# Sparse attention: probabilities times values as plain float32 products of 64 columns, in place of pairs of split fp32r products

## The chip, the cores and the metric

The kernel runs on one core of one Trainium2 chip. The metric is the device time of one execution in microseconds (us); three runs of the kernel before gave 2080.49, 2083.45 and 2084.88 us, so its median is 2083.45 us.

## The reference

Two blocks of a transformer are computed one after the other on 512 tokens of width 1024, in float32. The change lies in the second block, in one of its two mixers, the sparse attention (`nsa_mixer`). It has 16 query heads of 64 columns in 4 groups of 4; the heads of a group share keys and values. Each head's output is the gated sum of three attentions:

- over 31 compressed blocks of keys and values (padded to 32),
- over the selected blocks,
- over a window of 512 positions.

With 512 tokens the second and third both reach all earlier positions, so the kernel computes both as full causal attentions of 512 by 512 with the same bias, each with its own keys and values:

```
p   = softmax(q @ k.T / 8 + bias, over the keys s <= t)
out = gate_cmp * p_cmp @ v_cmp + gate_sel * p_sel @ v_sel + gate_win * p_win @ v_win
```

The other mixer (RWKV), the merge gates, the first block, the cross attention and the feed-forward networks are not touched.

## The kernel before, in words

Everything is held transposed: 128 channels on the partitions, 512 tokens along the free axis. Nearly every product that needs float32 accuracy is made on TensorE with the type fp32r, from operands that are split into a high part, rounded to fp32r by a ScalarE copy, and a low part, the rest, made by a VectorE subtraction. A weight product is then three fp32r matmuls: high by high, high by low, low by high (`gemm_g`, L243 to L245). Some small products are plain float32 matmuls instead: the bias tables (L973), the compression (L1013, L1097), the RWKV products (L744, L757, L874 to L891). Each of these shows as two matmul instructions in the trace; a transpose (L328) or an fp32r product shows as one.

The program is a number of phases. The one that matters here is called `pa2`; in the trace it runs from about 1050 to about 1500 us. Three generators are woven into one program order by `weave` (L57): each yields an estimate of its work, and the stream that is least far along goes next. The streams of `pa2` are the sparse attention (`nsa`), the RWKV chain with the merge behind it (`right`), and the last ten tiles of the merge gates (`merge_gates`, matmuls into `psg_m`). The yields, and so the weave, stand outside the edited lines. After that the build's scheduler moves instructions past each other on each engine; the order in the trace is therefore not that of the text (transposes of tile j+1 stand ahead of products of tile j, for instance). Each engine and each DMA queue then works strictly in the order that was built. When the attention stream has ended, the product of its output with a weight (`branch`, `psg_b`) follows, then the rest of the network.

The parts that the change touches:

- `nsa_compressed` (L1058, in the phase before) makes the compressed keys and values. The values stand in `vc`, for each of 4 groups 64 columns high part and 64 columns low part (L1098 on ScalarE, L1099 on VectorE).
- `nsa_pre` (L1112) makes, one group ahead, the queries, the keys of the selected branch, and the probabilities of the compressed branch. These are transposed on TensorE (L1150) and split into `pc`, high and low (L1151, by `split`, L162 and L163).
- `nsa_values` (L1155) loads, once for every two groups, the values of both branches: four transfers from `vd` into `ld` buffers, of which there are three, shared with the loads of queries and keys. ScalarE and VectorE then write the high and low parts side by side into `VT` (L1163, L1164), of which there is one buffer. The transfers are issued from GpSimd's queue (POOL), as are those of the bias (L1183), the queries and keys (L1052, L292) and the gates' weights (L209).
- `nsa_group` (L1166) runs 4 heads. A head starts its PSUM accumulator `o` (one bank) with two fp32r products of the compressed branch, 32 rows by 128 columns, 512 moving columns (L1188), and runs `attend` twice.
- `attend` (L299) is called by the sparse attention with a `gate` (32 times) and by the first block's attention without one (8 times). It makes the scores of four row blocks (L311, L312), adds the bias and takes the minimum on VectorE (L313), the exponential on ScalarE (L315), and scales the rows (L321, L323). Then, for each key tile j of 0 to 3, it transposes the probabilities (L328), copies them out of PSUM as fp32r (L330, ScalarE), subtracts for the low part (L331, VectorE) and multiplies both with `V(j)`, 128 stationary columns of which 64 are the value's high part and 64 its low part (L332, L333). The moving operand has 512, 384, 256 and 128 columns for the four j.
- `o_evac` (L335) adds the lower half of the accumulator to the upper: a ScalarE copy (L340) and a VectorE add (L341).

Of the kernel before, what the change touches and what calls it, by code (L numbers as in the profile page):

```python
# [8 lines left out]
F32 = mybir.dt.float32  # L9
# [29 lines left out]
class Gen:  # L39
# [259 lines left out]
    def attend(self, qst, kst, bias, V, o, first, last, gate=None):  # L299

        nc = self.nc
        kh, kl = kst
        st = self.f("sm", shape=(128, 32))
        m, s, r = st[:, 0:4], st[:, 4:8], st[:, 8:12]
        Pt = self.f("p", shape=(128, 1280))
        P = [Pt[:, 64 * i * (i + 1):64 * (i + 1) * (i + 2)] for i in range(4)]
        for i, pt in enumerate(P):
            w = 128 * (i + 1)
            ps = self.ps("a")
            qt = qst[:, i * 128:i * 128 + 128]  # L310
            nc.tensor.matmul(ps[:, :w], qt, kh[:, :w], start=True, stop=False)  # L311
            nc.tensor.matmul(ps[:, :w], qt, kl[:, :w], start=False, stop=True)  # L312
            nc.vector.tensor_tensor_reduce(pt, ps[:, :w], bias[:, 512 - w:], 1.0, 3e38, OP.add, OP.min,  # L313
                                           m[:, i:i + 1])
            nc.scalar.activation(pt, pt, AF.Exp, bias=m[:, i:i + 1], scale=-1.0, accum_out=s[:, i:i + 1])  # L315
        nc.vector.reciprocal(r, s)
        if gate is not None:
            nc.vector.tensor_tensor(r, r, gate, OP.mult)
        for i, pt in enumerate(P):
            if i >= 2:  # L320
                nc.scalar.activation(pt, pt, AF.Copy, scale=r[:, i:i + 1])  # L321
            else:
                nc.vector.tensor_scalar(pt, pt, r[:, i:i + 1], None, op0=OP.mult)  # L323
        for j in range(4):
            w = 512 - 128 * j
            ps = self.ps("b")
            for i in range(j, 4):
                nc.tensor.transpose(ps[:, (i - j) * 128:(i - j + 1) * 128], P[i][:, j * 128:j * 128 + 128], self.ident)  # L328
            ph, pl = self.f("pt", F32R), self.f("pt", F32R)
            nc.scalar.copy(ph[:, :w], ps[:, :w])  # L330
            nc.vector.tensor_tensor(pl[:, :w], ps[:, :w], ph[:, :w].bitcast(F32), OP.subtract)  # L331
            nc.tensor.matmul(o[:, j * 128:], V(j), ph[:, :w], start=first and j == 0, stop=False)  # L332
            nc.tensor.matmul(o[:, j * 128:], V(j), pl[:, :w], start=False, stop=last and j == 3)  # L333
# [724 lines left out]
    def nsa_compressed(self):  # L1058
        nc, A, V, S = self.nc, self.A, self.nc.vector, self.nc.scalar
        k = lambda n, w: self.rp.tile([128, w], F32R, name=n, tag=n, bufs=1)  # L1060
        self.cmp = kc2, vc = (k("kch", 128), k("kcl", 128)), k("vc", 512).rearrange("p (g s d) -> p g s d", g=4, s=2)
        self.gt = self.rp.tile([128, 4, 48], F32, name="gt", tag="gt", bufs=1)
        self.nsa_consts()
        yield 3.0
# [30 lines left out]
        for g in range(4):  # L1095
            for ct in range(2):
                nc.tensor.matmul(p[:, g], hx[ct][:, 128 * g:128 * g + 128], w2[:, ct, 128:192], start=ct == 0, stop=ct == 1)  # L1097
        S.copy(vc[:, :, 0], p)  # L1098
        V.tensor_tensor(vc[:, :, 1], p, vc[:, :, 0].bitcast(F32), OP.subtract)  # L1099
        yield 1.0  # L1100

    def norm_col(self, sq):
# [9 lines left out]
    def nsa_pre(self, g):  # L1112
# [35 lines left out]
        ps = self.ps("b")  # L1148
        for i in range(4):
            nc.tensor.transpose(ps[:, i * 128:i * 128 + 128], e[:, i * 128:i * 128 + 128], self.ident)  # L1150
        pc = self.split(ps, tag="pc")  # L1151
        yield 2.0
        return qst, kst, pc

    def nsa_values(self, gp):  # L1155
        nc, V, S = self.nc, self.nc.vector, self.nc.scalar
        VT = self.VT = self.f("vt", F32R, (128, 4 * 4 * 128)).rearrange("p (t k n) -> p t k n", t=4, k=4)
        for t2 in range(2):
            z = self.f("ld").rearrange("p (t k d) -> p t k d", t=2, d=64)
            for t in range(2):  # L1160
                self.side.dma_start(z[:, t].rearrange("p k d -> p (k d)"), self.vd[gp, 2 * t2 + t])
            v = VT[:, 2 * t2:2 * t2 + 2]
            S.copy(v[:, :, :, 0:64], z)  # L1163
            V.tensor_tensor(v[:, :, :, 64:128], z, v[:, :, :, 0:64].bitcast(F32), OP.subtract)  # L1164

    def nsa_group(self, g, qst, kst, pc):  # L1166

# [7 lines left out]
        for h in range(4):  # L1175
# [8 lines left out]
                                              ap=[[576, 2], [-1, 64], [1, 512]]))  # L1184
            o = self.ps("o")
            hs = slice(32 * h, 32 * h + 32)
            for i in range(2):
                nc.tensor.matmul(o, vc[hs, g].rearrange("p s d -> p (s d)"), pc[i][hs], start=i == 0, stop=False)  # L1188
            ready = self.nsa_pre(g + 1) if h == 3 and g < 3 else iter(())
            for br in (1, 2):  # L1190
                kv = 2 * (br - 1) + gl
# [3 lines left out]
                if br == 1:  # L1195
                    try:
# [1 line left out]
                            yield next(ready)  # L1198
                    except StopIteration as done:
                        pre = done.value  # L1200
            self.o_evac(O, o, par)
            if par == 1:
                pr = hd // 2
                nc.sync.dma_start(self.ynd[pr], O)
# [238 lines left out]
def emit(tc, A, out, dbg={}):  # L1443
    nc = tc.nc
    with ExitStack() as ctx:
# [14 lines left out]
        with g.phase("rec"):  # L1460
# [11 lines left out]
                g.weave(("", g.rwkv_fronts(xs), 245), ("_p", others(), 170))  # L1472
            g.banks = {"a": "01", "b": "23", "n": "2", "o": "4", "a_b": "5", "b_b": "6", "g_m": "7", "g_b": "56"}
            g.side = nc.gpsimd
            with g.phase("pa2", f=3, ld=3, qst=5, kst=6, p=2, pt=4, bias=2, pc=2, kz=1, o=1, ot=1, vt=1,
                         kb=1, v=1, bk=1, ys=1, vs=2, vu=2, yc=6, vgb=2, y=2, f_m=1, **{"as": 1}):
                g.reserve(kb=1024, v=512, vs=1024, vu=1024, yc=128, bk=1024, y=1024, ys=1024,
                          vgb=512, ld=512, kst=512, vt=2048, qst=512, f=512, pc=512, bias=512)

                live = {"", "_m"}  # L1480

# [146 lines left out]
```

## Time and profile before

| what | value |
|---|---|
| runs (us) | 2080.49, 2083.45, 2084.88; median 2083.45 |
| profiled execution | 2082.19 us, span of its instructions 2080.4 us |
| mean granted TensorE clock | 0.981 of full speed |
| TensorE matmul, busy | 2004.5 us (96%) |
| VectorE, busy | 1308.6 us (63%) |
| ScalarE, busy | 925.3 us (44%) |

The profile names the engines PE (TensorE matmul), PEld (its weight loads), DVE (VectorE), ACT (ScalarE), POOL (GpSimd) and SP (the queue that issues most transfers). Times are in us, means of single instructions in ns. Matmuls are pipelined: one may start while the one before still counts as busy, so the distance between two starts tells more of TensorE's load than the busy time. `128*128 128x512 f32` is a matmul with 128 rows and 128 columns of stationary operand and 512 moving columns; the trace writes f32 for fp32r operands of matmuls as well.

### The profile page before, as it was taken

The page shows a single profiled execution, that of the slowest core. Times are in us where ns is not written, and L with a number is a line of the kernel's source. Part 1 is how long each engine was busy: PE and PEld are TensorE (multiplying, and loading weights), DVE is VectorE, ACT ScalarE, POOL GpSimd, SP SyncE. Part 2 cuts the span into 40 slices and gives each one's busy share as a digit, 9 for nine tenths or more (in the row PEclk, how much of TensorE's full clock was granted, in tenths as well). Part 3 has the DMA queues.
Part 4 walks back from the last instruction along what each step waited for, and adds up shares of the span by engine and source line. Part 5 has one row for each costly group of instructions (what it writes and reads, how often), then busy time and mean ns, then how long its engine had stood idle before and what let it go on. Part 6 is the DMA issues. An engine that isn't in the chain of part 4 may idle for free.

```text
span 2080.4 us, 27852 instructions
## 1 busy us (share of the span) xinstructions
PE 2004.5 (96%) x9927; PEld 1627.0 (78%) x9927; DVE 1308.6 (63%) x3007; ACT 925.3 (44%) x1778; POOL 95.5 (5%) x167
## 2 busy tenths in 40 slices
PE   8999999999999899899988899999999999999999
PEld 7778888888888677777767687887878778888887
DVE  5785432554463568687848988888466756666522
ACT  4874531442254233333346577777243443333311
POOL 0000000000003200000120111000000000000000
PEclk9999999999999999999989899999999999999999
DMA  5222332333355754755673445446442123333332
GB/s 161 82 85 93 99 93 92 117 108 120 117 185 158 171 147 141 183 147 168 191 168 105 129 122 145 126 123 190 154 140 84 41 81 92 101 92 98 95 109 84
DMA packets 178267, 256.75 MB, mean 123 GB/s; under 512 B 95409, under 2 KB 109953, under 8 KB 178129
## 3 DMA queue, kind: packets, MB, share of 16 engines
q1 hardware_dynamic: 162832, 231.31, 38.2%
q0 software_dynamic: 15296, 23.66, 3.9%
q8 instruction: 79, 1.29, 0.3%
q14 instruction: 60, 0.48, 0.1%
HBM read 205.12 MB, written 45.53 MB: 120 GB/s over the span
## 4 chain that ended last, share of the span: by engine, by line
PE 46%; DVE 6%; ACT 3%; issue 2%; DMA 2%; SPq 0%; POOL 0%; DVEq 0%; ACTq 0%; POOLq 0%
PE psg L243 8%; PE psg L245 8%; PE psg L244 8%; PE psg_b L243 1%; PE psg_b L244 1%; PE psg_b L245 1%; PE psb L328 1%; DVE ys L777 1%; PE psg_p L243 1%; PE psg_p L244 1%; PE psg_p L245 1%; PE pso L332 1%; PE psa L744 1%; DVE ys L778 1%; PE pso L333 1%
## 5 line engine op out<-in xcount | busy, mean ns | idle before, releaser
L222 ACT CAST wh<-ws 128x1024 fp32r<-128x1024 f32 (+2 forms) x283 | 291.6, 1031 | 697.9 <-PE psg L244 457.1
L223 DVE TENSOR_TENSOR wl<-ws,wh 128x1024 fp32r<-128x1024 f32 (+2 forms) x283 | 339.4, 1201 | 266.3 <-ACT wh L222 265.7
L243 PE MATMUL psg<-xh,wh 128*128 128x512 f32 x984 | 392.2, 399 | 4.7 <-ACT wh L222 4.7
L245 PE MATMUL psg<-xh,wl 128*128 128x512 f32 x984 | 393.1, 399 | 0.0
L244 PE MATMUL psg<-act,wh 128*128 128x512 f32 x912 | 359.7, 395 | 1.1 <-DVE act L166 1.1
L243 PEld LDWEIGHTS psg<-xh,wh 128*128 128x128 f32 x984 | 186.0, 189 | 46.8 <-ACT wh L222 5.5
L245 PEld LDWEIGHTS psg<-xh,wl 128*128 128x128 f32 x984 | 186.0, 189 | 41.5 <-issue 1.2
L244 PEld LDWEIGHTS psg<-act,wh 128*128 128x128 f32 x912 | 171.1, 188 | 42.8 <-DVE act L166 1.5
L243 PE MATMUL psg<-act,wh 128*128 128x512 f32 x496 | 196.1, 397 | 2.8 <-ACT act L165 1.4
L245 PE MATMUL psg<-act,wl 128*128 128x512 f32 x496 | 196.1, 396 | 0.5 <-DVE wl L223 0.5
L244 PE MATMUL psg<-xl,wh 128*128 128x512 f32 x352 | 139.7, 397 | 0.0
L243 PEld LDWEIGHTS psg<-act,wh 128*128 128x128 f32 x496 | 92.8, 188 | 27.2 <-ACT act L165 2.2
L245 PEld LDWEIGHTS psg<-act,wl 128*128 128x128 f32 x496 | 93.0, 187 | 23.7 <-DVE wl L223 1.3
L315 ACT ACTIVATE p<-p,sm 128x128 f32<-128x128 f32 (+3 forms) x160 | 89.6, 561 | 15.0 <-DVE sm L313 13.6
L331 DVE TENSOR_TENSOR pt<-psb,pt 128x512 fp32r<-128x512 f32 (+3 forms) x160 | 75.8, 487 | 20.0 <-ACT pt L330 17.7
L244 PE MATMUL psg<-x,wh 128*128 128x512 f32 x216 | 88.2, 409 | 0.0
L313 DVE CUSTOM_DVE_ANT_0 p<-psa,bias 128x128 f32<-128x128 f32 (+3 forms) x160 | 75.9, 485 | 8.2 <-PE psa L312 6.1
L328 PE MATMUL psb<-ident,p 128*128 128x128 f32 x400 | 75.3, 285 | 2.5 <-DVE y L921 0.9
L244 PEld LDWEIGHTS psg<-xl,wh 128*128 128x128 f32 x352 | 66.3, 188 | 14.0
L330 ACT CAST pt<-psb 128x512 fp32r<-128x512 f32 (+3 forms) x160 | 65.8, 424 | 25.7 <-PE psb L328 20.8
L243 PE MATMUL psg_p<-xh,wh 128*128 128x512 f32 x176 | 73.3, 416 | 1.1 <-ACT f L957 0.6
L244 PE MATMUL psg_p<-x,wh 128*128 128x512 f32 x176 | 72.2, 410 | 0.0
(491 smaller groups left out, 3899.1 us busy)
## 6 DMA issues: line engine op xcount, KB each, us to landing
ws<-in_w_in SPq DMA_DIRECT2D x49, 512.0 KB, 4.0
ws<-in_w_fup SPq DMA_DIRECT2D x44, 512.0 KB, 3.5
ws<-in_w_up SPq DMA_DIRECT2D x32, 512.0 KB, 3.5
ws<-in_w_down SPq DMA_DIRECT2D x32, 512.0 KB, 3.6
ws<-in_w_fdn SPq DMA_DIRECT2D x16, 512.0 KB, 3.6
ws<-in_w_qku SPq DMA_DIRECT2D x12, 512.0 KB, 3.6
ws<-in_w_in POOLq DMA_DIRECT2D x10, 512.0 KB, 4.6
ws<-in_w_out SPq DMA_DIRECT2D x8, 512.0 KB, 3.5
```

What stands on the lines that cost most here:

```text
L222: nc.scalar.copy(wh[:, :n], ws[:, :n])
L223: nc.vector.tensor_tensor(wl[:, :n], ws[:, :n], wh[:, :n].bitcast(F32), OP.subtract)
L243: nc.tensor.matmul(p[:, :n], wh[:, s], h[:, :n], start=c + k == 0, stop=False)
L244: nc.tensor.matmul(p[:, :n], wh[:, s], l[:, :n], start=False, stop=False)
L245: nc.tensor.matmul(p[:, :n], wl[:, s], h[:, :n], start=False, stop=last)
L313: nc.vector.tensor_tensor_reduce(pt, ps[:, :w], bias[:, 512 - w:], 1.0, 3e38, OP.add, OP.min, m[:, i:i + 1])
L315: nc.scalar.activation(pt, pt, AF.Exp, bias=m[:, i:i + 1], scale=-1.0, accum_out=s[:, i:i + 1])
L328: nc.tensor.transpose(ps[:, (i - j) * 128:(i - j + 1) * 128], P[i][:, j * 128:j * 128 + 128], self.ident)
L330: nc.scalar.copy(ph[:, :w], ps[:, :w])
L331: nc.vector.tensor_tensor(pl[:, :w], ps[:, :w], ph[:, :w].bitcast(F32), OP.subtract)
L332: nc.tensor.matmul(o[:, j * 128:], V(j), ph[:, :w], start=first and j == 0, stop=False)
L333: nc.tensor.matmul(o[:, j * 128:], V(j), pl[:, :w], start=False, stop=last and j == 3)
```

## The change

In the gated attentions the transposed probabilities are copied out of PSUM once, as float32, and multiplied with the 64 value columns in one plain float32 product for each j, into the lower 64 partitions of `o`. The values are loaded straight into `VT`, without a split; the compressed branch's probabilities and values are not split either, and its two products become one. The two halves of the accumulator are no longer added; one ScalarE copy empties it. The buffers follow: `vt` 1024 words instead of 2048, `vc` 256 instead of 512, one `pc` instead of two, two `o` instead of one, and no `ot`. The first block's attention, called without a gate, stays as it was.

```diff
--- before.py
+++ after.py
@@ -326,6 +326,11 @@
             ps = self.ps("b")
             for i in range(j, 4):
                 nc.tensor.transpose(ps[:, (i - j) * 128:(i - j + 1) * 128], P[i][:, j * 128:j * 128 + 128], self.ident)
+            if gate is not None:
+                pf = self.f("pt")
+                nc.scalar.copy(pf[:, :w], ps[:, :w])
+                nc.tensor.matmul(o[:64, j * 128:], V(j), pf[:, :w], start=first and j == 0, stop=last and j == 3)
+                continue
             ph, pl = self.f("pt", F32R), self.f("pt", F32R)
             nc.scalar.copy(ph[:, :w], ps[:, :w])
             nc.vector.tensor_tensor(pl[:, :w], ps[:, :w], ph[:, :w].bitcast(F32), OP.subtract)
@@ -1058,7 +1063,7 @@
     def nsa_compressed(self):
         nc, A, V, S = self.nc, self.A, self.nc.vector, self.nc.scalar
         k = lambda n, w: self.rp.tile([128, w], F32R, name=n, tag=n, bufs=1)
-        self.cmp = kc2, vc = (k("kch", 128), k("kcl", 128)), k("vc", 512).rearrange("p (g s d) -> p g s d", g=4, s=2)
+        self.cmp = kc2, vc = (k("kch", 128), k("kcl", 128)), k("vc", 256).bitcast(F32).rearrange("p (g d) -> p g d", g=4)
         self.gt = self.rp.tile([128, 4, 48], F32, name="gt", tag="gt", bufs=1)
         self.nsa_consts()
         yield 3.0
@@ -1095,8 +1100,7 @@
         for g in range(4):
             for ct in range(2):
                 nc.tensor.matmul(p[:, g], hx[ct][:, 128 * g:128 * g + 128], w2[:, ct, 128:192], start=ct == 0, stop=ct == 1)
-        S.copy(vc[:, :, 0], p)
-        V.tensor_tensor(vc[:, :, 1], p, vc[:, :, 0].bitcast(F32), OP.subtract)
+        S.copy(vc, p)
         yield 1.0
 
     def norm_col(self, sq):
@@ -1148,20 +1152,15 @@
         ps = self.ps("b")
         for i in range(4):
             nc.tensor.transpose(ps[:, i * 128:i * 128 + 128], e[:, i * 128:i * 128 + 128], self.ident)
-        pc = self.split(ps, tag="pc")
+        pc = self.f("pc")
+        S.copy(pc, ps)
         yield 2.0
         return qst, kst, pc
 
     def nsa_values(self, gp):
-        nc, V, S = self.nc, self.nc.vector, self.nc.scalar
-        VT = self.VT = self.f("vt", F32R, (128, 4 * 4 * 128)).rearrange("p (t k n) -> p t k n", t=4, k=4)
-        for t2 in range(2):
-            z = self.f("ld").rearrange("p (t k d) -> p t k d", t=2, d=64)
-            for t in range(2):
-                self.side.dma_start(z[:, t].rearrange("p k d -> p (k d)"), self.vd[gp, 2 * t2 + t])
-            v = VT[:, 2 * t2:2 * t2 + 2]
-            S.copy(v[:, :, :, 0:64], z)
-            V.tensor_tensor(v[:, :, :, 64:128], z, v[:, :, :, 0:64].bitcast(F32), OP.subtract)
+        VT = self.VT = self.f("vt", shape=(128, 4 * 4 * 64)).rearrange("p (t k d) -> p t k d", t=4, k=4)
+        for t in range(4):
+            self.side.dma_start(VT[:, t].rearrange("p k d -> p (k d)"), self.vd[gp, t])
 
     def nsa_group(self, g, qst, kst, pc):
 
@@ -1184,8 +1183,7 @@
                                               ap=[[576, 2], [-1, 64], [1, 512]]))
             o = self.ps("o")
             hs = slice(32 * h, 32 * h + 32)
-            for i in range(2):
-                nc.tensor.matmul(o, vc[hs, g].rearrange("p s d -> p (s d)"), pc[i][hs], start=i == 0, stop=False)
+            nc.tensor.matmul(o[:64], vc[hs, g], pc[hs], start=True, stop=False)
             ready = self.nsa_pre(g + 1) if h == 3 and g < 3 else iter(())
             for br in (1, 2):
                 kv = 2 * (br - 1) + gl
@@ -1198,7 +1196,7 @@
                             yield next(ready)
                     except StopIteration as done:
                         pre = done.value
-            self.o_evac(O, o, par)
+            nc.scalar.copy(O[64 * par:64 * par + 64], o[:64])
             if par == 1:
                 pr = hd // 2
                 nc.sync.dma_start(self.ynd[pr], O)
@@ -1472,10 +1470,10 @@
                 g.weave(("", g.rwkv_fronts(xs), 245), ("_p", others(), 170))
             g.banks = {"a": "01", "b": "23", "n": "2", "o": "4", "a_b": "5", "b_b": "6", "g_m": "7", "g_b": "56"}
             g.side = nc.gpsimd
-            with g.phase("pa2", f=3, ld=3, qst=5, kst=6, p=2, pt=4, bias=2, pc=2, kz=1, o=1, ot=1, vt=1,
+            with g.phase("pa2", f=3, ld=3, qst=5, kst=6, p=2, pt=4, bias=2, pc=1, kz=1, o=2, vt=1,
                          kb=1, v=1, bk=1, ys=1, vs=2, vu=2, yc=6, vgb=2, y=2, f_m=1, **{"as": 1}):
                 g.reserve(kb=1024, v=512, vs=1024, vu=1024, yc=128, bk=1024, y=1024, ys=1024,
-                          vgb=512, ld=512, kst=512, vt=2048, qst=512, f=512, pc=512, bias=512)
+                          vgb=512, ld=512, kst=512, vt=1024, qst=512, f=512, pc=512, bias=512)
 
                 live = {"", "_m"}
```

## Rows read from the trace of the kernel before

**Rows 1.** The page, its span and part 1: busy us of each engine.

```profile
span 2080.4 us, 27852 instructions
PE 2004.5 (96%) x9927; PEld 1627.0 (78%) x9927; DVE 1308.6 (63%) x3007; ACT 925.3 (44%) x1778; POOL 95.5 (5%) x167
```

**Rows 2.** Timeline of PE, 1429 to 1432: start us, us, engine, line, operation.

```profile
1429.23 0.39 PE L243 MATMUL psg_b<-y,wh 128*128 128x512 f32 x1
1429.46 0.39 PE L244 MATMUL psg_b<-kb,wh 128*128 128x512 f32 x1
1429.69 0.34 PE L333 MATMUL pso<-pt,vt 128*128 128x384 f32 x1
1429.87 0.27 PE L328 MATMUL psb<-ident,p 128*128 128x128 f32 x1
...
1430.79 0.28 PE L333 MATMUL pso<-pt,vt 128*128 128x256 f32 x1
1430.92 0.22 PE L332 MATMUL pso<-pt,vt 128*128 128x128 f32 x1
1430.98 0.28 PE L333 MATMUL pso<-pt,vt 128*128 128x128 f32 x1
1431.09 0.30 PE L328 MATMUL psb<-ident,p 128*128 128x128 f32 x1
```

**Rows 3.** Stretches: us, busy (instructions) of PE, PEld, DVE, ACT, POOL, PEclk, DMA share, GB/s.

```profile
1087.00:1200.00 113.00, 98.07 (x555) 80.86 (x553) 97.53 (x324) 70.03 (x202) 10.45 (x16) 0.89 0.47 121
1200.00:1425.00 225.00, 216.32 (x1352) 177.85 (x1352) 189.05 (x655) 170.37 (x480) 18.81 (x29) 1.00 0.51 140
1425.00:1450.00 25.00, 24.97 (x134) 19.72 (x133) 22.40 (x60) 22.51 (x55) 0.00 (x0) 0.97 0.43 132
1450.00:1530.00 80.00, 80.00 (x346) 64.11 (x344) 39.02 (x48) 16.63 (x19) 0.00 (x0) 1.00 0.50 151
```

**Rows 4.** Groups of PE by shape, 1200 to 1425: busy us, mean ns, idle before.

```profile
L243 PE MATMUL psg_m<-xh,wh 128*128 128x512 f32 x55 | 23.4, 425 | 0.0
L332 PE MATMUL pso<-pt,vt 128*128 128x384 f32 x20 | 7.4, 372 | 1.1 <-ACT pt L330 1.1
L1188 PE MATMUL pso<-pc,vc 32*128 32x512 f32 x18 | 7.1, 455 | 0.1
L1125 PE MATMUL psa<-qst,kz 128*128 128x512 f32 x16 | 5.1, 420 | 0.0
```

**Rows 5.** Plain float32: line L973, then PE's timeline around it and in L1013.

```profile
L973 PE MATMUL psb<-f,tab x10: 188/587/597, 682.2 to 698.7; 32*16 32x512 f32 x6, 32*16 32x32 f32 x2, 32*16 32x128 f32 x2
...
681.83 0.40 PE L245 MATMUL psg<-xh,wl 128*128 128x512 f32 x1
682.16 1.89 PE L973 MATMUL psb<-f,tab 32*16 32x512 f32 x4
683.97 0.50 PE L243 MATMUL psg<-xh,wh 128*128 128x512 f32 x1
684.31 0.39 PE L244 MATMUL psg<-x,wh 128*128 128x512 f32 x1
...
756.77 1.50 PE L1013 MATMUL psb<-blk,cw 128*128 128x128 f32 x12
```

**Rows 6.** Timeline of PE around a pair of L1188.

```profile
1255.85 0.39 PE L881 MATMUL psa_b<-rb,vs 128*128 128x128 f32 x2
1256.16 0.73 PE L1188 MATMUL pso<-pc,vc 32*128 32x512 f32 x2
1256.82 0.49 PE L874 MATMUL psb_b<-vs,ws 128*128 128x128 f32 x2
```

**Rows 7.** Groups of DVE, 1055 to 1460: busy us, mean ns, idle before.

```profile
L331 DVE TENSOR_TENSOR pt<-psb,pt 128x512 fp32r<-128x512 f32 (+3 forms) x128 | 60.9, 488 | 16.7 <-ACT pt L330 15.0
L341 DVE TENSOR_TENSOR o<-pso,ot 64x512 f32<-64x512 f32 x16 | 11.0, 686 | 1.2 <-ACT ot L340 0.8
```

**Rows 8.** Waits, 1200 to 1425: who for whom, us in total, times, longest.

```profile
PEld pso L332 <- ACT pt L330: 9.2, 29, 0.8
PEld pso L333 <- DVE pt L331: 4.4, 11, 1.7
```

**Rows 9.** The value loads of L1161, and the timeline where the second values come.

```profile
DMA to landing us min/median/max: 3.6/7.1/7.9
...
1286.77 0.22 PE L333 MATMUL pso<-pt,vt 128*128 128x128 f32 x1
1289.85 0.59 POOL L1052 DMA_DIRECT2D ld<-qd  x1 [13.82 <-DVE vt L1164]
1291.49 0.50 PE L332 MATMUL pso<-pt,vt 128*128 128x512 f32 x1
```

**Rows 10.** Timeline of PE at 769, where L561 waits.

```profile
769.34 0.38 PE L561 MATMUL psn<-blk,f 128*128 128x2 f32 x2 [3.43 <-DVE vc L1099]
```

## The prediction

> **What bounds the kernel now.** I read the page first, then the busy time by stretches of the sparse-attention stage, then groups by shape, waits, and single steps in the timeline. The page [rows 1] shows TensorE busy for 96% of the span, but a busy matmul is not a full slot: a 512-column product lasts 0.39 us, and the next starts 0.23 us after it began [rows 2]. So I count starts, not busy time.
>
> The change acts between 1087 and 1450 us, where the 32 gated attentions run beside the RWKV stream and the merge gates. Three stretches differ [rows 3]. In A (1087 to 1200, 8 attentions) VectorE is busy for 97.5 of 113 us. In B (1200 to 1425, 20 attentions) PE issues 1352 products in 225 us. In C (1425 to 1450, 4 attentions) PE is full, and behind it, to 1530 us, stand only weight products, with PE full again: whatever PE does in C is paid in time.
>
> How full is PE in B? 512-column products [rows 4]: 166 for the gates (L243 has 55, the like rows of L244 and L245 55 and 56), 4 in each of 20 attentions (L311, L312, L332 and L333; 20 by the row of 384 columns), 18 of L1188, 16 of L1125: 280. Steps [rows 2]: 0.23 us for 512 columns, 0.18 for 384, 0.13 for 256; for a small one I take 0.11 (the run of twelve in [rows 5]). So 280 x 0.23 + 80 x 0.18 + 80 x 0.13 + 912 x 0.11 = 189.5 us, and 9 pairs of L1188 lose 0.39 us each (below): 193 of 225 us, 86%. In A I take the mean step of B (193/1352 = 0.143): 555 x 0.143 = 79 us at full clock, and about 89 at the granted 0.89. B is near PE's limit; A is VectorE's.
>
> **The change, part by part.**
>
> *The value products.* Before, each of the four key tiles j has two fp32r products; the steps above with 0.09 for 128 columns (0.06 and 0.11 in [rows 2]) give 2 x (0.23 + 0.18 + 0.13 + 0.09) = 1.26 us per attention. Plain float32 products already stand in the trace: L973's five products show as ten instructions, so each issues two, and four of 512 columns in a row take 1.89 us, the last 0.59 of it: a step of (1.89 - 0.59)/3 = 0.43 us [rows 5]. Only 16 columns are stationary there, so narrowness buys nothing. At 128 columns twelve such instructions take 1.50 us, a step of 0.11 [rows 5]. Scaled by columns between them: 2 x (0.43 + 0.325 + 0.22 + 0.11) = 2.17 us. That adds 0.91 us per attention, 29 us over 32. L1188 becomes one product in two instructions of 0.43 where two of 0.23 stood: 0.40 us for each of 16 heads, 6.4 us.
>
> *The change of array shape.* In [rows 5] PE goes from 128 x 128 products to 32 x 16 ones and back. The first starts 0.33 us after the product before it, not 0.23; the last of the four starts 3 x 0.43 after 682.16, at 683.46, and the next product 0.51 later (683.97), not 0.43; and that one's successor comes 0.34 behind it, not 0.23. Sum 0.29 to 0.31 us. Around a pair of L1188 [rows 6] the same count gives 0.09 on entry, 0.66 instead of 0.46 inside and on leaving, and 0.10 behind: 0.39. No row has 128 rows with 64 columns, so the price of one such visit lies between 0 and 0.39 us. I take 0.31, since [rows 5] are nearest, being plain float32 with fewer columns. Products of adjacent j can share a visit, as products of two j stand together in [rows 2] (1430.79 to 1430.98); I let one in four share: 0.93 us per attention, 30 in all. The Trainium skill, TensorEngine Tiling (Array Packing), Key Properties, says that changing the tiling mode drains TensorE, and its list of configurations has 128 x 64 as a mode of its own; no run here shows that mode, and by that rule the term stands, without it the term is 0.
>
> *VectorE.* Gone are the 128 subtractions L331 (60.9 us), the 16 adds L341 (11.0) [rows 7], and, costed at L341's 0.69 us, four subtractions each of L163 for pc and of L1164: some 77 us, of which 8 x 1.90 + 4 x 0.69 = 18 in A. ScalarE keeps its copies, and loses only the four of nsa_values. What waits shortens: L333 waited for L331 [rows 8], and between heads L1188 waits for one copy, not for copy and add. What is late next is the ScalarE copy L330, on which L332 waits longest already [rows 8].
>
> *The value load.* The eight transfers stay on POOL's queue, but now write VT itself, of which there is one. Those of the second pair of groups cannot start before the last product of head 7 (1286.77); landing takes 3.6 to 7.9 us, and head 8's first value product ran at 1291.49 [rows 9]. Behind these four on POOL's queue stand bias, query and gate-weight loads, and behind a late product everything on PE. Against that, the ld buffers are free: POOL waited 13.82 us for one [rows 9]. Landed at 7.9 us after three more issues of some 0.56, the last tile is there at 1296, 5 us late; twice that if the queue behind waits too. If it lands at 3.6 us nothing is late, and the loads behind that wait gain some 5. Bounds: -5 to +10; I take +3, as the tiles are needed one after another.
>
> *Elsewhere.* Without L1099 the PSUM bank for L561 comes free earlier; PE waited 3.43 us there [rows 10], but the next weights are late too: 0 to -3.4, I take -1. The second o buffer, the single pc buffer and the smaller tiles I cost at 0: pc is read last when a group's fourth head begins (L1188), before the next group's pc is made in that same head, and the some 20 us of a head (10 heads in the 225 us of B) cover that; uncovered it would be one wait of a copy's length per group.
>
> *Sum.* Each attention adds 0.91 + 0.93 = 1.84 us of PE, each head 0.40. B: 193 + 20 x 1.84 + 9 x 0.40 = 233.4 us. With VectorE relieved PE should be filled better than 86% but not fully; I take 95%, near what C does: 246 us, +21. A: 89 + 8 x 1.84 + 4 x 0.40 = 105, at 95% 111 of 113: -2, VectorE's 18 us being eaten by PE. C: 4 x 1.84 + 2 x 0.40 = +8. With +3 and -1: **+29 us**. The profiled execution took 2082.19 us (span 2080.4), 1.26 below the median of 2083.45; on the median: **2112 us**.
>
> **The rivals.**
> *No drain for 64 columns.* For: no row shows a shape that differs in columns alone. Against: both changes of shape in [rows 5, 6] pay. Then A 89 + 7.3 + 1.6 = 98, at 95% 103 (-10); B 193 + 18.2 + 3.6 = 215, 226 (+1); C +4.4; with +2: about -2, **2081 us**.
> *VectorE paces the stage (faster).* If no visit costs anything and the subtraction was the true brake, A gives back all of VectorE's 18 us, and B runs at 98%: 215/0.98 = 219 (-6); C +4; the load is hidden: about -20, **2063 us**. For: A's 86% on VectorE and its queue of small RWKV steps behind L331. Against: B's 86% on PE. It decides once PE fills over 95% of B and visits cost under 0.05 us.
> *Heavier.* Every product its own visit at 0.39 us (2.47 us per attention) and PE filled to 93%: B 246/0.93 = 264 (+39), A 110/0.93 = 119 (+6), C +11, load and queue +5: **2144 us**.
>
> **How the numbers follow.** Forecast 58%, no drain 19%, VectorE 12%, heavier 11%. The range 2072 to 2140 leaves out the VectorE case and part of the heavier one; the forecast alone would span 2096 to 2130. A difference under 0.2%, 4.2 us, can't be told from none. Faster: 12% and a third of the no-drain case, 18%; same: about half of that case, 10%; slower 72%.
>
> **What would show it.** Right: value products in two instructions each, 0.43 us apart at 512 columns; the start before and behind one late by about 0.1 us each, with the next weights loaded late; VectorE's busy time down by about 77 us, PE with no more idle than 5% in B; A about as long as before, B some 20 us and C some 8 us longer; nothing changed before 680 us and behind the stage. Wrong: a step into a 64-column product as short as between equals (no drain), A shorter by 10 us or more (VectorE), or a stall of over 10 us at head 8 behind POOL's value loads.

## The result, and the profile after

The changed kernel takes 2095.15 us (median of 5 runs, 2092.22 to 2099.27) where the kernel before took 2080.99 beside it (5 runs, 2079.99 to 2084.88). The ratio is 1.0066, with a 95% interval of 1.0047 to 1.0085: slower by some 14 us. The forecast was 2112, 29 us slower, with a range of 2072 to 2140. The direction and the range held; the size was twice too large.

First the page of the changed kernel (busy time, share of the span, instructions), against [rows 1]:

```profile
PE 2035.7 (97%) x9927; PEld 1603.2 (77%) x9927; DVE 1246.0 (60%) x2854; ACT 923.9 (44%) x1774; POOL 95.1 (5%) x167
```

VectorE is busy for 62.6 us less, where the forecast had named about 77 as a sign of being right. The 153 instructions that went lasted 79 us taken one by one, but neighbours on VectorE overlap by about 0.09 us each (a 0.69 us instruction is followed by the next after 0.60), and busy time counts an overlap once. TensorE is busy for 31 us more.

Now the three stretches of [rows 3] again (us, then busy time and instructions of PE, PEld, DVE, ACT, POOL, then PEclk, DMA share, GB/s):

```profile
1087.00:1200.00 113.00, 109.56 (x623) 77.58 (x622) 90.48 (x303) 78.66 (x230) 12.71 (x20) 0.98 0.53 136
1200.00:1425.00 225.00, 221.16 (x1248) 156.96 (x1247) 135.59 (x520) 152.83 (x431) 15.59 (x24) 0.99 0.44 120
1425.00:1450.00 25.00, 22.06 (x93) 12.24 (x92) 12.79 (x39) 18.86 (x49) 0.00 (x0) 0.93 0.51 159
```

In the first stretch TensorE starts 623 products where it started 555, and its granted clock is 0.98, not 0.89: it idles less, so it spends less time at the lower level. In the second it starts 1248 instead of 1352 in the same 225 us, though VectorE has over a quarter less to do there (135.6 us for 189.1). Equal clock times hold different work, however, so the comparison needs landmarks. I take the start of the last projection product of the stage ahead (psg_p), the instruction that brings a head's output out of PSUM (L341 before, L1199 after) for heads 3, 13 and 15, and the last product of psg_b. The changed kernel, from its timeline (start, duration, engine, line):

```profile
1038.60 0.39 PE L245 MATMUL psg_p<-xh,wl 128*128 128x512 f32 x1
...
1176.96 0.58 ACT L1199 COPY o<-pso 64x512 f32<-64x512 f32 x1 [0.41 <-PE pso L332]
...
1428.64 0.58 ACT L1199 COPY o<-pso 64x512 f32<-64x512 f32 x1
...
1460.66 0.58 ACT L1199 COPY o<-pso 64x512 f32<-64x512 f32 x1
...
1542.79 0.40 PE L245 MATMUL psg_b<-p,wl 128*128 128x512 f32 x1
```

The same landmarks of the kernel before:

```profile
1048.70 0.39 PE L245 MATMUL psg_p<-xh,wl 128*128 128x512 f32 x1
...
1189.24 0.69 DVE L341 TENSOR_TENSOR o<-pso,ot 64x512 f32<-64x512 f32 x1
...
1426.37 0.69 DVE L341 TENSOR_TENSOR o<-pso,ot 64x512 f32<-64x512 f32 x1 [0.44 <-ACT ot L340]
...
1450.32 0.69 DVE L341 TENSOR_TENSOR o<-pso,ot 64x512 f32<-64x512 f32 x1
...
1529.75 0.40 PE L245 MATMUL psg_b<-p,wl 128*128 128x512 f32 x1
```

The differences of these starts, beside the forecast's terms (e3 is an experiment, below):

| stretch | before | after | difference | forecast | e3, 128 columns |
|---|---|---|---|---|---|
| up to the last psg_p product | 1048.7 | 1038.6 | -10.1 | -1 | 1036.0 |
| heads 0 to 3 (A) | 140.5 | 138.4 | -2.1 | -2 | 137.0 |
| heads 4 to 13 (B) | 237.1 | 251.7 | +14.6 | +21, and +3 for the value load | 247.3 |
| heads 14 and 15 (C) | 24.0 | 32.0 | +8.0 | +8 | 33.6 |
| to the last psg_b product | 79.4 | 82.1 | +2.7 | 0 | 82.0 |
| to the end of the span | 550.7 | 550.6 | 0 | 0 | 552.2 |

The attention stage lost 23 us, not far from the 30 forecast for it. Each column is one execution. A second profile of the changed kernel (a0 below, an execution of 2086.31 us) has 1034.6, 134.7, 251.5, 30.9, 82.1 and 550.6, so the first two rows differ by some 4 us between executions of one kernel, the others by about 1, and the stage lost 18 us there. The larger miss lies ahead of that stage, where the change touches a single VectorE instruction.

### The profile page after: what moved, and what is told of

It reads as the page before. It is cut to its first block, busy times and chain, and to the rows that moved or that the text cites. A ratio compares the mean times of both kernels' runs of the same rounds, so it can differ in the third digit from the quotient of the medians.

```text
span 2093.4 us, 27672 instructions
## 1 busy us (share of the span) xinstructions
PE 2035.7 (97%) x9927; PEld 1603.2 (77%) x9927; DVE 1246.0 (60%) x2854; ACT 923.9 (44%) x1774; POOL 95.1 (5%) x167
## 4 chain that ended last, share of the span: by engine, by line
PE 48%; DVE 6%; DMA 4%; ACT 3%; issue 3%; SPq 0%; POOL 0%; DVEq 0%; POOLq 0%; ACTq 0%
PE psg L243 9%; PE psg L245 9%; PE psg L244 8%; PE pso L332 3%; PE psg_b L244 1%; PE psg_b L243 1%; DVE ys L782 1%; PE psg_b L245 1%; PE psb L328 1%; PE psa L749 1%; DVE ys L783 1%; DVE wl L223 1%; DMA vu<-vs 1%; PE pso L1186 1%; PE psa L311 1%
## 5 line engine op out<-in xcount | busy, mean ns | idle before, releaser
L244 PE MATMUL psg<-act,wh 128*128 128x512 f32 x912 | 359.7, 395 | 1.1 <-DVE act L166 1.1
L244 PEld LDWEIGHTS psg<-act,wh 128*128 128x128 f32 x912 | 171.0, 188 | 42.9 <-DVE act L166 1.5
L244 PE MATMUL psg<-xl,wh 128*128 128x512 f32 x352 | 139.7, 397 | 0.0
L332 PE MATMUL pso<-pt,vt 128*64 128x512 f32 (+3 forms) x256 | 86.3, 454 | 5.1 <-ACT pt L331 4.8
L244 PE MATMUL psg<-x,wh 128*128 128x512 f32 x216 | 89.2, 413 | 0.0
L244 PEld LDWEIGHTS psg<-xl,wh 128*128 128x128 f32 x352 | 66.3, 188 | 14.3
L245 PE MATMUL psg_p<-xh,wl 128*128 128x512 f32 x176 | 71.6, 408 | 0.0
L244 PE MATMUL psg_p<-x,wh 128*128 128x512 f32 x176 | 71.2, 405 | 0.0
```

Source lines behind the costliest of these rows:

```text
L244: nc.tensor.matmul(p[:, :n], wh[:, s], l[:, :n], start=False, stop=False)
L245: nc.tensor.matmul(p[:, :n], wl[:, s], h[:, :n], start=False, stop=last)
L332: nc.tensor.matmul(o[:64, j * 128:], V(j), pf[:, :w], start=first and j == 0, stop=last and j == 3)
```

## The experiments

All ratios are to the kernel before on the same chip, with their 95% intervals. The changed kernel, run again beside one set of them, repeated its ratio:

> The changed kernel itself, unchanged, on the same chip as the other runs of this set, so that they can be set against it. Every theory: 1.0066 of the kernel before, 1.0047 to 1.0085.

Measured: 2095.44 us against 2081.11; 1.0065 (1.0045 to 1.0085).

### What happened ahead of the stage: L1099

**e1**, the changed kernel with that subtraction back:

```diff
-        S.copy(vc, p)
+        S.copy(vc[:, :, 0], p)
+        V.tensor_tensor(vc[:, :, 1], p, vc[:, :, 0], OP.subtract)
```

> The changed kernel, with the subtraction that made the low part of the compressed values (L1099 of before, 0.41 us on VectorE) put back behind the copy in nsa_compressed; its result is used by nothing. Every engine then issues the compressed-value stage and the projections (up to about 1050 us) in the order of before, and the attention stage in the order of the changed kernel. Theory 1 (the changed kernel won some 10 us before the attention stage because VectorE's order behind that subtraction changed, and lost some 23 us in the attention stage): 2105 us, about 10 above the changed kernel, with the last projection of the RWKV front (psg_p) ending at about 1049 us as in before. Rival (the 10 us are chance, such as clock or transfer times of that execution, or come from the smaller buffers of the next stage): 2095 us, psg_p ends at about 1039.

Measured: 2106.70 us; 1.0107 (1.0087 to 1.0127). The last psg_p product starts at 1048.98, as theory 1 has it, and the ratio is 0.0041 to 0.0042 (some 8.7 us) above the two of the changed kernel. The changed kernel itself was not run beside e1, however. e4 (below), which was, and which has no such subtraction, lies only 0.0010 under it in time, though its last psg_p product starts at 1038.85. So the place of the loss rests on the traces, and its size on the next two runs.

**e5**, the same from the other side, in the kernel before. The low part of the compressed values is left out:

```diff
-        V.tensor_tensor(vc[:, :, 1], p, vc[:, :, 0].bitcast(F32), OP.subtract)
+        S.activation(vc[:, :, 1], p, AF.Copy, scale=0.0)
```

> The kernel before, with the low part of the compressed values not computed: ScalarE fills it with zeros, so VectorE has no subtraction L1099. All else, the split value products too, is that of before. Theory 1 (that subtraction's place in VectorE's order costs some 10 us before the attention stage): about 2071 us, psg_p ends at about 1039 us instead of 1049. Rival (the 10 us belong to something else): 2081 us.

Measured: 2078.79 us against 2085.37; 0.9961 (0.9945 to 0.9977), 8 us faster. Its last psg_p product starts at 1043.62, between the two values named.

**e2**, the low part made on GpSimd, nothing left out:

```diff
-        V.tensor_tensor(vc[:, :, 1], p, vc[:, :, 0].bitcast(F32), OP.subtract)
+        f = self.f("f")[:, :256].rearrange("p (g d) -> p g d", g=4)
+        S.copy(f, p)
+        nc.gpsimd.tensor_tensor(vc[:, :, 1], f, vc[:, :, 0].bitcast(F32), OP.subtract)
```

> The kernel before, with the low part of the compressed values made on GpSimd from a copy by ScalarE, so that nothing is left out; VectorE has no subtraction L1099. Theory 1 (as in e5, its place in VectorE's order costs some 8 us): about 8 us under the kernel before, 0.996 of it. Rival (any change there only reshuffles the order, by chance for better or worse): between 0.995 and 1.005.

Measured: 2074.73 us; 0.9967 (0.9949 to 0.9984), 7 us faster. The ratio lies within the band that the rival allowed as well, so this run by itself tells nothing apart; with e5 it is the second edit of the kernel before with the same sign and much the same size.

Why is one short instruction worth that much? The timeline of the kernel before around it, VectorE (DVE) and TensorE:

```profile
766.62 0.09 DVE L769 MEMSET as<- 128x32 f32 x1 [5.58 <-DMA as<-adr]
...
768.87 0.41 DVE L1099 TENSOR_TENSOR vc<-psb,vc 128x256 fp32r<-128x256 f32 x1
...
769.34 1.05 PE L561 MATMUL psn<-blk,f 128*128 128x2 f32 x8 [3.43 <-DVE vc L1099]
...
773.01 0.63 PE L244 MATMUL psg<-x,wh 128*128 128x512 f32 x1
773.43 0.63 PE L245 MATMUL psg<-xh,wl 128*128 128x512 f32 x1
...
776.54 0.60 PE L573 MATMUL psn<-ident,cx 128*128 128x128 f32 x4
...
777.17 0.75 DVE L719 SCALAR_TENSOR_TENSOR f<-rkv,vt,psn 128x512 f32<-128x512 f32 x1 [2.25 <-PE psn L573]
```

And that of the changed kernel, where L566, L578 and L724 are the L561, L573 and L719 of before:

```profile
759.98 0.95 PE L566 MATMUL psn<-blk,f 128*128 128x2 f32 x8
...
762.10 0.09 DVE L774 MEMSET as<- 128x32 f32 x1 [5.89 <-DMA as<-adr]
...
767.84 0.66 PE L578 MATMUL psn<-ident,cx 128*128 128x128 f32 x4 [0.43 <-ACT cx L575]
...
768.54 0.75 DVE L724 SCALAR_TENSOR_TENSOR f<-rkv,vt,psn 128x512 f32<-128x512 f32 x1
```

VectorE works in order. Before, L1099 stood behind a memset that waited 5.58 us for a transfer, and until L1099 had read its PSUM bank TensorE did not start L561. So L561 ran 2.7 us after the transfer had let VectorE go (769.34 - 766.62). After the change ScalarE alone empties the bank, and the same products run 2.1 us before that point (762.10 - 759.98). Their result goes through small column steps on VectorE and a copy by ScalarE to L573, and from there to L719. Before, though, L573 does not wait for that copy. TensorE issues 20 products of 512 columns without a gap between L561 and L573, and eight of them, after it had idled for 3.43 us, at steps of 0.39 to 0.43 us and not 0.23; the granted clock is the last number but two of this row:

```profile
771.00:774.00 3.00, 3.00 (x9) 2.33 (x8) 3.00 (x31) 1.04 (x3) 0.00 (x0) 0.54 0.35 87
```

After the change 16 stand between the two, none at such a step, so TensorE's order has moved as well. From VectorE's release to L719 it was 10.6 us, and to L724 it is 6.4. By the last psg_p product the lead, counted from the same release, is 5.6 us: 282.1 before and 276.5 after. In e1, whose order in this stretch is that of before, it is 283.7 (from 765.24 to 1048.98), 7.2 us more than after. All fourteen profiles agree: in the two with L1099 on VectorE it is 282.1 and 283.7, in the twelve without it 270.4 to 277.4, 274.3 in the mean. What the earlier release, the moved order and the clock each gave is not separated: in e2 L719 comes 9.0 us after VectorE's release, only 1.5 sooner than before, and the last psg_p product 8.0 us sooner. The other 4.5 us of the 10.1 stand ahead of the release, where both kernels issue in the same order; they are a difference between executions, in which the release falls between 762.1 and 766.6 us.

### What the change of shape costs

**e3** uses the pair of neighbouring heads, which already lie side by side, as a 128-column stationary operand, and reads the half that is wanted:

```diff
-                nc.tensor.matmul(o[:64, j * 128:], V(j), pf[:, :w], ...
+                nc.tensor.matmul(o[:, j * 128:], V(j), pf[:, :w], ...
...
-                kv = 2 * (br - 1) + gl
+                kv = slice(2 * br - 2, 2 * br)
...
-            nc.scalar.copy(O[64 * par:64 * par + 64], o[:64])
+            nc.scalar.copy(O[64 * par:64 * par + 64], o[64 * gl:64 * gl + 64])
```

> The changed kernel with every value product made 128 columns wide: the stationary operand is the pair of neighbouring value heads that already lie side by side, and the half of the result that belongs to the other head is not read. The same number of products, passes and moved columns, and the same order on every engine; only the change of array shape around the value products of 128 rows is gone (that of the 32-row product L1186 stays). Theory 1 (a visit to 64 columns drains TensorE for about 0.3 us; some 70 such visits stand in the changed kernel): 0.3 x 70 = 21 us less, about 2074 us, which is under the kernel before. Rival (the visits are hidden or the cost is the two passes per product alone): 2095 us, and steps into and out of these products as long as before.

Measured: 2091.62 us against 2085.37; 1.0033 (1.0019 to 1.0047), 7 us under the changed kernel by the ratios. (Under e4, which was run beside it, it is 13.) Theory 1 asked for 21, the rival for none. The timelines of the same stretch of work show why. TensorE in the changed kernel:

```profile
1249.38 0.48 PE L244 MATMUL psg_m<-x,wh 128*128 128x512 f32 x1
1249.79 1.72 PE L332 MATMUL pso<-pt,vt 128*64 128x512 f32 x4
1251.44 0.55 PE L328 MATMUL psb<-ident,p 128*128 128x128 f32 x3
1251.82 0.39 PE L884 MATMUL psa_b<-wh,vu 128*128 128x128 f32 x2
1252.05 0.39 PE L886 MATMUL psa_b<-rb,vs 128*128 128x128 f32 x2
1252.36 0.86 PE L332 MATMUL pso<-pt,vt 128*64 128x256 f32 x4
1253.16 0.49 PE L879 MATMUL psb_b<-vs,ws 128*128 128x128 f32 x2
1253.48 0.38 PE L1134 MATMUL psb<-ident,f 128*128 128x128 f32 x2
```

The same in e3:

```profile
1244.60 0.48 PE L244 MATMUL psg_m<-x,wh 128*128 128x512 f32 x1
1244.97 1.77 PE L332 MATMUL pso<-pt,vt 128*128 128x512 f32 x4
1246.58 0.49 PE L328 MATMUL psb<-ident,p 128*128 128x128 f32 x3
1246.90 0.39 PE L884 MATMUL psa_b<-wh,vu 128*128 128x128 f32 x2
1247.13 0.39 PE L886 MATMUL psa_b<-rb,vs 128*128 128x128 f32 x2
1247.42 0.92 PE L332 MATMUL pso<-pt,vt 128*128 128x256 f32 x4
1248.17 0.39 PE L879 MATMUL psb_b<-vs,ws 128*128 128x128 f32 x2
1248.40 0.38 PE L1134 MATMUL psb<-ident,f 128*128 128x128 f32 x2
```

From L244 to the L884 behind the first group it is 2.44 us after and 2.30 in e3; from L886 to L1134 around the second, 1.43 and 1.27. Removing the shape saves 0.14 and 0.16 us, half of a visit's price. The start into the group comes hardly sooner (0.41 and 0.37; 0.31 and 0.29), since the product then waits for something else. The waits of TensorE on the copy say what. First the changed kernel, then e3 (total us, times, longest; 1080 to 1460):

```profile
PE pso L332 <- ACT pt L331: 4.8, 9, 2.0
```

```profile
PE pso L332 <- ACT pt L331: 8.3, 14, 3.8
```

Both kernels place the value products in 74 groups, 54 of four instructions (two key tiles) and 20 of two. I summed, over all of them, by how much the starts lie further apart than the shortest steps (0.43, 0.32, 0.215 and 0.109 us for value products; 0.2315 for other 512-column products; for smaller ones 0.018 us plus the columns over 2400 per us, at least 0.06):

| excess, us | into the group | inside it | first start behind | the next one | sum | ratio |
|---|---|---|---|---|---|---|
| changed kernel, 64 columns | 16.8 | 5.2 | 7.4 | 8.1 | 37.5 | 1.0066 |
| e3, 128 columns | 17.3 | 7.1 | 0.4 | 3.3 | 28.1 | 1.0033 |
| e7, 128 columns, copies shared | 8.7 | 6.7 | -0.6 | 4.1 | 18.9 | 1.0004 |
| e7b, 64 columns, copies shared | 12.2 | 5.2 | 7.0 | 8.1 | 32.4 | 1.0045 |

The entry and the inside cost nothing net (22.0 us with 64 columns, 24.4 with 128), and the longest wait there is that for ScalarE's copy; what differs is the exit, 15.5 us and 3.7. **e7** and **e7b** test that reading. In both, VectorE takes half of the copies; e7 starts from e3, e7b from the changed kernel, and the instruction order is the same in both:

```diff
-                nc.scalar.copy(pf[:, :w], ps[:, :w])
+                (nc.vector.tensor_copy if j % 2 else nc.scalar.copy)(pf[:, :w], ps[:, :w])
```

> The kernel of e3 (128 columns) with the copies of key tiles j = 1 and 3 (L331) on VectorE instead of ScalarE. Theory C (in e3 TensorE waits at the start of a group of value products for the ScalarE copies, which is why taking the drain away there won nothing: the excess ahead of the 74 groups was 16.8 us in the changed kernel and 17.3 in e3): the excess ahead of and inside the groups falls from 24.4 us in e3 to some 16, and the kernel is 5 us or more under e3, 0.998 to 1.001 of the kernel before. Rival (that wait comes from the order of the transposes, not from the copy's engine): the same as e3, 1.0033, with the excess unchanged.

Measured: 2082.24 us against 2081.95; 1.0004 (0.9981 to 1.0027). The excess into and inside the groups fell from 24.4 to 15.4 us, and the wait on the copy to this:

```profile
PE pso L332 <- ACT pt L331: 1.0, 4, 0.3
```

The wait, the excess and the time came out as theory C has them. Two things stay open: the intervals of e3 and e7 overlap, and the built order of e7 is another than e3's, on TensorE too, so the rival (the order of the transposes) is not shut out.

> The same sharing of the copies in the changed kernel itself (64 columns); order as in the run beside it. Theory C: with the copies sooner the drain that the copy had covered shows in full, so the distance between 64 and 128 columns grows from 0.0033 of the time (7 us) to 0.006 or more (12 to 20 us): 1.005 to 1.008 of the kernel before. Rival (the drain costs what it costs, 7 us, whatever the copy does): 0.0033 above the run beside it.

Measured: 2091.77 us; 1.0045 (1.0027 to 1.0063). The distance between 64 and 128 columns is 0.0041 (some 8.5 us) where it was 0.0033. In the excess it grew from 9.4 to 13.5 us, as theory C has it, but in time the growth is smaller than it asked for and lies within the intervals. That more of the drain is paid in time once the copies are shared is not shown.

### What the doubled products cost

**e6** keeps e3's shape and takes one fp32r pass; the low parts of probabilities and values are left out:

```diff
-                pf = self.f("pt")
+                pf = self.f("pt", F32R)
...
-        VT = self.VT = self.f("vt", shape=(128, 4 * 4 * 64))...
+        VT = self.VT = self.f("vt", F32R, (128, 4 * 4 * 64))...
```

> The kernel of e3 (value products 128 columns wide, no change of shape) with the value products in one fp32r pass instead of plain float32: probabilities and values are taken as fp32r without their low parts, which leaves those parts out of the result. The order of the attention stage shifts with it. By the steps inside these products (0.43, 0.323, 0.216 and 0.109 us an instruction, two each) a plain attention takes 2.16 us and one in fp32r about 0.63, so 1.53 us less in each of 32, 49 us of TensorE time. Theory A (TensorE's time in the stage is the bound, so the doubled length of the plain products is what the stage lost): e3 minus most of 49 us, about 2050 us. Theory B (the stage is held by the chain of waits, above all by the ScalarE copy L331 ahead of each product, and TensorE's extra time is half hidden): 2070 us or more, with longer waits on L331 in the profile.

Measured: 2059.04 us against 2081.11; 0.9885 (0.9860 to 0.9910), 31 us under e3 by the ratios. That is two thirds of the 49 us that TensorE saves, between the two theories. Theory B's longer waits on L331 aren't there (3.5 us in all). The order also shifts in this run, so the two thirds are a rough figure.

### The value load at head 8

**e4** gives the values two tiles, so that the reload doesn't wait:

```diff
-  ... o=2, vt=1,
+  ... o=2, vt=2,
```

> The changed kernel with two tiles for the values (vt=2; the space is that of the one wide tile of before), so that the four value loads of the second pair of groups need not wait for the last product of head 7. The order on every other engine is unchanged. Theory 1 (the reload costs about 3 us at head 8, whose distance to head 7 was 21 us where heads 6 and 7 were 19 us apart): 2092 us. Rival (the wait is covered by the RWKV stream and the gates): 2095 us within 1.

Measured: 2106.01 us against 2085.37; 1.0097 (1.0078 to 1.0117). Nothing is gained: heads 4 to 13 take 252.6 us in e4 and 251.7 in the changed kernel. The changed kernel's timeline shows that the reload costs nothing:

```profile
1274.38 2.17 POOL L1163 DMA_DIRECT2D vt<-vd  x4 [0.30 <-PE pso L332]
...
1285.15 1.72 PE L332 MATMUL pso<-pt,vt 128*64 128x512 f32 x4
```

The four transfers are issued from 1274.38 on, and in this stretch they land in this time (the shortest, the median and the longest):

```profile
DMA to landing us min/median/max: 4.0/4.3/4.7
```

So the last tile is there by about 1281, 4 us before head 8 wants it. Why e4 came out 0.003 above the changed kernel is known in part. The two intervals overlap by a hair, and only the places of the four loads in POOL's queue differ. In the profiles e4 is 4.7 us longer, and 2.8 of these lie behind the stage (553.4 us for 550.6), where both issue the same instructions and the granted clock differs. The ten microseconds from about 2 us behind the last psg_b product, in e4 and then in the changed kernel:

```profile
1547.00:1557.00 10.00, 8.92 (x27) 6.84 (x26) 7.08 (x14) 5.21 (x13) 0.00 (x0) 0.66 0.68 223
```

```profile
1545.00:1555.00 10.00, 8.92 (x39) 6.92 (x38) 9.83 (x19) 7.94 (x19) 0.00 (x0) 1.00 0.72 222
```

e1, run beside e4, shows the same (0.66, and 2.8 us), and e3 some of it (0.83, and 1.6 us). So part of what e1 and e4 have over the changed kernel is not their edit's.

### A kernel that beats both

If A belongs to VectorE and B to TensorE, plain products should be used in A alone. **e8** is e2 with plain products for the first group's eight attentions; the wide tile of high and low parts is read as float32, so the shape stays:

```diff
+            if plain:
+                pf = self.f("pt")
+                nc.scalar.copy(pf[:, :w], ps[:, :w])
+                nc.tensor.matmul(o[:, j * 128:], V(j).bitcast(F32), pf[:, :w], ...
+                continue
...
-  False, br == 2, gate=self.gt[:, :, 3 * hd + br])
+  False, br == 2, gate=self.gt[:, :, 3 * hd + br], plain=g == 0)
```

> The kernel of e2 with plain float32 value products for the first group alone (8 of 32 attentions, those of the stretch in which VectorE is busiest, 1087 to 1200 us), and with the wide stationary tile of before read as float32, so 128 columns and no change of shape; the other 24 attentions keep the split. It takes 8 x 4 subtractions, 8 x 1.90 = 15 us, off VectorE there and adds 8 x 0.91 = 7 us to TensorE. Theory (that stretch is VectorE's): some 8 us under e2, 0.992 of the kernel before. Rival (the chain of waits holds that stretch too): the same as e2, 0.996.

Measured: 2066.42 us; 0.9916 (0.9892 to 0.9940), 0.0051 (11 us) under e2, where 8 were expected. The stretch that holds most of group 0, in e2 and then in e8:

```profile
1085.00:1195.00 110.00, 95.96 (x521) 79.20 (x520) 92.55 (x300) 65.45 (x190) 10.46 (x16) 0.84 0.44 115
```

```profile
1085.00:1195.00 110.00, 101.11 (x592) 81.07 (x591) 89.26 (x298) 71.77 (x207) 11.62 (x18) 0.95 0.50 123
```

TensorE starts 592 products instead of 521 in the same time, and its granted clock rises from 0.84 to 0.95. The stretch gains twice over: less waiting for VectorE, and with less idling less time at 1.2 GHz. The two are not separated, but the clock is no chance of one execution: from the last psg_p product to head 3's output it is 0.85 to 0.88 in the three profiles whose first group has split products (before, e5, e2) and 0.91 to 0.95 in the other eleven. In these two profiles heads 0 to 3 take 6.2 us less in e8, and heads 4 to 13, which the edit leaves alone, 4.9 less; why those gain is not shown.

**e11** goes one group further (`plain=g < 2`), **e12** makes the narrowest product plain in every gated attention (`if plain or gate is not None and j == 3:`):

> The kernel of e8 with plain value products in the first two groups (16 of 32 attentions). The second group runs in the stretch where TensorE is fuller (1189 to 1288 us in before). Theory (the split pays where TensorE is the fuller engine, the plain product where VectorE is): slower than e8, by about a third of the 24 us that separate e3 from e8, so 0.995 of the kernel before. Rival (plain pays as long as the shape does not change, and e3 lost by something else): 0.988 or less.

Measured: 2073.35 us; 0.9947 (0.9928 to 0.9966), 0.0031 above e8. The intervals overlap a little, but heads 4 to 13 take 241.5 us where they took 233.4 in e8: in the second group the plain product loses, as the theory has it.

> The kernel of e8 with the narrowest value product (key tile j = 3, 128 columns) plain in all gated attentions. It takes 24 subtractions of 0.285 us off VectorE, 6.8 us, and adds 2 x (0.109 - 0.07) = 0.08 us to TensorE for each, 2 us. Theory (a narrow plain product is nearly free on TensorE): 0 to 4 us under e8, 0.990 to 0.992 of the kernel before. Rival (VectorE has slack in those stretches, and any added TensorE time is paid): 0.992 to 0.993.

Measured: 2064.18 us; 0.9915 (0.9892 to 0.9938), no different from e8, and too near to both expectations to tell them apart. e8 and e12 beat both kernels, by 17 to 18 us against the one before.

## Why the prediction was right in direction and twice too large

**The failed step is "Elsewhere", -1 us.** It named the right place: L1099 holds the PSUM bank for L561, and TensorE waits 3.43 us there [rows 10]. But it took that idle time as the upper bound. The idle time of TensorE is what TensorE itself lost; L561 moved by more, from 2.7 us behind VectorE's release to 2.1 us ahead of it. What follows it moved too: the chain through VectorE, ScalarE and TensorE back to VectorE, into the RWKV front, TensorE's own order, and its clock behind the idle time. e5 and e2 put the term at -8 and -7 us, and the fourteen profiles at some 8.6 from VectorE's release to the last psg_p product (274.3 for 282.9 in the mean). Of the 15 us between forecast and result this is nearly half, 6 to 7.

**The visits were right in kind, too many, and their cover was overlooked.** In the trace a visit delays the product that enters by 0.09 us, the one inside by 0.05 (0.48 instead of 0.43 between two 512-column ones), the start behind by 0.09 and the next by 0.05: 0.29 us, where 0.31 was taken. The Trainium skill's rule on this (TensorEngine Tiling (Array Packing), Key Properties), that a change of the tiling mode drains TensorE, holds here for 128 rows by 64 columns too. But the new order places the key tiles in pairs, so there are 74 groups and not 96. With 0.67 us in place of 0.93 per attention, the forecast's B sum is 233.4 - 20 x 0.26 = 228.2 us, at the forecast's own 95% 240, and +15 instead of +21: what was measured (+14.6).

**That this fits is partly luck.** e3 shows that without any visit to 64 columns the stage still loses 19 us (499.9 against 481.0), 16 of them in the three stretches, where the rival "no drain" expected these to win 5 together. And the visits, 74 x 0.29 = 21 us of TensorE, cost 7 by e3 and 8.5 by e7 and e7b. Both speak against one assumption, that TensorE would be filled to 95% in either case. Some of the drain stands where TensorE would wait for the ScalarE copy; take the drain away, and the wait stays. In the forecast the copy was named as "late next" and given no price. By e7 it is some 6 us in e3 (0.0029 of the time), with the new order in it.

**The value products** were costed exactly: 0.43, 0.32, 0.215 and 0.109 us an instruction, 2.15 us per attention for 2.17 forecast. By e6 their length is the stage's main loss: two thirds of the 29 us that they add would be 19, what e3's stage lost.

**A and C** came out as forecast, -2 and +8, but not by the forecast's reasons. A's clock rose from 0.89 to 0.98, which the forecast did not name; with 79/0.98 = 81 us in place of its 89 the sum at 95% would have ended 9 us lower, at -11, and the second profile of the changed kernel has -6. In C, e3 without the visits loses more, 9.7 us, and with the copies shared e7 and e7b lose 3.8 and 4.4: the visits did not make the +8, and half of it goes with the copies.

**The value load**, +3 us, cost nothing: it lands 4 us early. The 2.7 us behind C, where nothing was forecast, stay unexplained.

**VectorE** was relieved of instructions of 79 us, where 77 were forecast, and the rival that it paced the whole stage is out: in e11 relief loses in the second group. For the first group e8 bears the rival out: relief of VectorE won there.

## What to carry to other kernels

Price a removed instruction by what its result, or the buffer that it frees, lets start, and follow that chain to the engine that sets the time; the idle time charged to it in the profile is one engine's share and no upper bound (here 3.43 us idle against 7 to 8 us of time). Look, too, whether the built order moves with it. An added delay on a busy engine is paid only where that engine would not have waited anyway, so look at what releases each instruction beside it before adding the delay up. And trade one engine's time for another's stretch by stretch: the plain product that won 11 us in the stretch where VectorE was busiest lost when the next group had it too.

## What was not expected of the hardware

That relief of VectorE would go with a higher granted clock of TensorE: 0.84 to 0.95 in 1085 to 1195 us between e2 and e8, with 71 more products started there, and 0.89 to 0.98 in A between the two kernels. And that a TensorE delay of 0.29 us, reckoned for each of 74 places, would be paid for in part only: 7 to 8.5 us of 21.
